# A decoder trunk on one core: the order of the small TensorE products in the RWKV tiles

## The chip, the core and the metric

The kernel runs on one core of a Trainium2 chip. The metric is device time in microseconds (us), the median of several executions. PE is TensorE, DVE is VectorE, ACT is ScalarE, POOL is GpSimd, and SP issues the DMAs.

## What is computed

Two layers on a residual stream of 256 tokens by 2048 channels: an RWKV-7 time mixing with a squared-ReLU MLP, then a latent attention with another MLP, each with norms and modulations made from a condition vector. The change lies in the time mixing. Cut to what matters, for each of 32 heads of 64 channels:

```python
def step(S, inp):
    r_t, w_t, k_t, v_t, kk_t, a_t = inp
    sa = jnp.einsum('bhvk,bhk->bhv', S, -kk_t)
    S = (S * w_t[:, :, None, :]
         + sa[..., None] * (kk_t * a_t)[:, :, None, :]
         + v_t[..., None] * k_t[:, :, None, :])
    y_t = jnp.einsum('bhvk,bhk->bhv', S, r_t)
    return S, y_t
```

The kernel does not walk the 256 tokens. It takes them in two chunks of 128, and within a chunk it solves for all the tokens at once: a triangular matrix of 128 by 128 per head and chunk is inverted, block by block.

## The kernel before

The program is one stream of Python calls; a planner in the framework orders each engine's instructions by their dependencies, its own estimate of times and the order of the calls, and puts the waits in. Each engine runs its list in that order.

**The RWKV stage** (here 230 to 754 us) runs 16 tiles, one for each pair of heads: `rwkv_tile(i)`, a generator whose yields are its steps. The loop at lines 905 to 928 keeps up to three tiles in flight, begins one every 9 steps, and between the steps draws the fill: the projections of the next tile (`project_rk`, lines 566 to 586: 48 products of 256 columns for each of two weight matrices go through `mm3w`, lines 213 to 215), and for the last tiles the first part of the output projection (`out_start`, lines 208 to 210). With every half of a weight tile that is loaded, ACT makes its high part (line 162), DVE its low part (line 163), and `pump` lets DVE do a share of the modulation sums of later layers (line 310). So PE's list in this stage mixes long projections with the many small products of the tiles.

A float32 product stands in the profile as two matrix instructions, called passes here. The steps of a tile that the change touches:

- `matrices` (lines 653 to 668), called twice for a tile, for `MB` and for `MK`: four products that contract over the 64 channels of one head. Head 0 lies on partitions 0 to 63, head 1 on 64 to 127; each head has a PSUM bank of its own (`pm[0]`, `pm[1]`, from the two banks of the pool `mm`). After them ACT copies head 0's bank, then head 1's (lines 663 and 666), with a mask by POOL between (line 667). Eight passes a group, 32 groups.
- the 32 by 32 blocks (lines 750 to 764): for each of four blocks of the diagonal four products, `A32` by `Tn` into `pW` (line 753), then `W` by `T16` into `pN` (line 762). The four blocks use four parts of the array (`tile_position=(32 * qi, 32 * qi)`) and four partition ranges of one bank; the block is the outer loop. 32 passes a group, 16 groups of each.
- the joins of two blocks (lines 773 to 788): for each half of the diagonal four products into `pW` (line 777) and a copy by ACT into `W32` (line 779), then four into `pN` (line 785) and a copy into `Tt` (line 787). The half is the outer loop, and the copy of the first half stands between the halves: both halves write one bank, and its next products come behind the copy. Eight passes a half.
- the state of the second chunk (lines 830 to 836): for each head two products into its 64 partitions of `psS` (lines 834 and 835), then a copy by ACT. Four passes a head.

Lines 793 to 806 (the 64 by 64 join), 825, 843 and 844 are not touched.

Of the kernel before, what the change touches and what calls it, by code (L numbers as in the profile page):

```python
# [20 lines left out]
P = 128  # L21
D = 2048
KT = D // P
T = 256
# [52 lines left out]
def trunk_kernel(ctx: ExitStack, tc: tile.TileContext, a, out, dbg=None):  # L77
    nc = tc.nc
    PE, DVE, ACT, POOL, SP = nc.tensor, nc.vector, nc.scalar, nc.gpsimd, nc.sync
# [52 lines left out]
    m16 = kc[:, o_ + 4 : o_ + 12]  # L132
    dlt = kc[:, o_ + 12 : o_ + 76].rearrange("p (m i) -> p m i", m=4)


    SEED, C0, C1 = 0x5F1FFFF9, 0.703952253, 2.38924456

# [216 lines left out]
    def big(name):  # L354
        return ap_.tile([P, 2, D], F32, tag="big", name=name)
# [22 lines left out]
    with ExitStack() as s0:  # L378
# [11 lines left out]
        with ExitStack() as s1:  # L390
# [5 lines left out]
            V = big("V")  # L396
# [28 lines left out]
            x = p2.tile([P, 2, D], F32, name="x")  # L425
# [36 lines left out]
            for cb in range(4):  # L462
# [13 lines left out]
                for kt in range(cb * 4, cb * 4 + 4):  # L476
# [8 lines left out]
                    h = p6.tile([P, T + 1], F32, tag="h", name="h")  # L485
# [4 lines left out]
                    for j in (3, 4, 5, 2, 0, 1):  # L490
# [10 lines left out]
                        if j == 3 or j == 4:  # L501
                            q = (kt % 4) * 2 * DL + (j - 3) * DL
                            wh, wl = lw_un["lwa"]
                            mm3w((pw if j == 3 else pa)[:DL], wh[:, q : q + DL], wl[:, q : q + DL], hi, lo, False, False)
                        elif j == 5:
                            q = (kt % 4) * 256
# [34 lines left out]
        with ExitStack() as s2:  # L541
# [9 lines left out]
            def tmp(tag, shape=(T,), bufs=1, dt=F32):  # L551
                return p5.tile([P, *shape], dt, tag=tag, name=tag, bufs=bufs)
# [8 lines left out]
            for j in range(LONG):  # L561
                Tt = p4.tile([P, 4, P], F32, name=f"Tt{j}")
# [25 lines left out]
            def rwkv_tile(i):  # L588
                K1 = DL + 1

                def tbank(name, k):
                    return banks[k].tile([P, 512], F32, tag=k, name=name)
# [7 lines left out]
                for z, (zh, zl) in enumerate(((zw_h, zw_l), (za_h, za_l))):  # L600
                    q = slice(z * P, (z + 1) * P)
# [34 lines left out]
                AR = tmp("AR", (2, 2, P), LONG)  # L636
# [14 lines left out]
                yield  # L651

                def matrices(lhs, M):
                    pm = [tbank("pm", "mm") for h in range(2)]
                    for c in range(2):
                        for h in range(2):
                            hp = slice(h * 64, h * 64 + 64)
                            PE.matmul(pm[h][:, c * T : (c + 1) * T], lhs[hp, c * P : (c + 1) * P],  # L658
                                      AR[hp, c, :, :].rearrange("p x t -> p (x t)"), start=True, stop=True)
                    for h in range(2):  # L660
                        if M is MB:
                            for c in range(2):
                                ACT.activation(M[:, h, c, :, :].rearrange("p x t -> p (x t)"), pm[h][:, c * T : (c + 1) * T],
                                               AF.Copy, scale=rinv[:, 2 * c + h : 2 * c + h + 1])
                        else:
                            ACT.copy(M[:, h].rearrange("p c x t -> p (c x t)"), pm[h])
                        POOL.affine_select(out=M[:, h], in_=M[:, h], pattern=[[0, 2], [1, 2], [1, P]], compare_op=ALU.is_ge,
                                           fill=0.0, base=-1, channel_multiplier=-1)

                MB = tmp("MB", (2, 2, 2, P), LONG)  # L670
                matrices(bt, MB)

                def At(m):
                    return MB[:, m // 2, m % 2, 0, :]
# [6 lines left out]
                bk = tmp("bk", bufs=2)  # L681
                for h in range(2):
                    q = slice(h * 64, h * 64 + 64)
# [4 lines left out]
                A32 = tmp("A32", (4, 32))  # L688
# [23 lines left out]

                MK = tmp("MK", (2, 2, 2, P), 2)
                matrices(kt_, MK)
                yield
                X = tmp("X", (4, 16), 2)
                ACT.copy(X, dlt)
                xt = tmp("xt", (4, 16))
                for j in range(15):
                    n = 15 - j  # L720
                    o = j * 16 + j + 1 if j < 8 else 128 + (j - 8) * 8 + j - 7
# [15 lines left out]
                for h in range(2):  # L737
                    vs = V[:, 0, i * P + h * 64 : i * P + h * 64 + 64]
# [3 lines left out]
                T16 = tmp("T16", (4, 32))  # L742
# [3 lines left out]
                quads = [slice(32 * q, 32 * q + 32) for q in range(4)]  # L746
                Tn = tmp("Tn", (4, 32))
                DVE.transpose(Tn.rearrange("p m t -> p (m t)"), T16.rearrange("p m t -> p (m t)"))
                yield
                pW = tbank("pW", "rt")  # L750
                for qi, q in enumerate(quads):
                    for m_ in range(4):
                        PE.matmul(pW[q, m_ * 16 : m_ * 16 + 16], A32[q, m_, :], Tn[q, m_, 0:16], start=True, stop=True,
                                  tile_position=(32 * qi, 32 * qi))
                W = tmp("W", (4, 32))
                POOL.memset(W[:, :, 16:32], 0.0)
                ACT.activation(W[:, :, 0:16], pW[:, 0:64].rearrange("p (m t) -> p m t", m=4), AF.Copy, scale=par[:, 1:2])
                yield
                pN = tbank("pN", "rt")
                for qi, q in enumerate(quads):  # L760
                    for m_ in range(4):
                        PE.matmul(pN[q, m_ * 32 : m_ * 32 + 32], W[q, m_, :], T16[q, m_, :], start=True, stop=True,
                                  tile_position=(32 * qi, 32 * qi))
                DVE.tensor_add(T16, pN[:, 0:P].rearrange("p (m t) -> p m t", m=4), T16)
                Tt = Tts[i % LONG]
                for q in quads:
# [2 lines left out]
                T32 = tmp("T32", (4, 32))  # L769
                W32 = T32  # L770
                DVE.transpose(T32.rearrange("p m t -> p (m t)"), T16.rearrange("p m t -> p (m t)"))
                yield
                pW = tbank("pW", "rt")
                for p_ in range(2):
                    e, o = slice(64 * p_, 64 * p_ + 32), slice(64 * p_ + 32, 64 * p_ + 64)
                    for m_ in range(4):
                        PE.matmul(pW[o, m_ * 32 : m_ * 32 + 32], At(m_)[e, o], T32[e, m_, :], start=True, stop=True,
                                  tile_position=(64 * p_, 64 * p_ + 32))
                    ACT.copy(W32[o], pW[o, 0:P].rearrange("p (m t) -> p m t", m=4))
                yield  # L780
                pN = tbank("pN", "rt")
                for p_ in range(2):
                    e, o = slice(64 * p_, 64 * p_ + 32), slice(64 * p_ + 32, 64 * p_ + 64)
                    for m_ in range(4):
                        PE.matmul(pN[e, m_ * 32 : m_ * 32 + 32], W32[o, m_, :], Tt[o, m_, o], start=True, stop=True,
                                  tile_position=(64 * p_ + 32, 64 * p_))
                    ACT.copy(Tt[e, :, o], pN[e, 0:P].rearrange("p (m t) -> p m t", m=4))
                yield

# [7 lines left out]
                pW = tbank("pW", "rt")  # L797
# [5 lines left out]
                pN = tbank("pN", "rt")  # L803
# [8 lines left out]
                for c in range(2):  # L812
                    if c:
                        pr = tbank("prhs", "rb")
                        PE.matmul(pr[:, :P], AR[:, c, 0, :], S, start=True, stop=False)
                        for h in range(2):
                            vs = V[:, c, i * P + h * 64 : i * P + h * 64 + 64]
                            PE.matmul(pr[:, h * 64 : h * 64 + 64], MK[:, h, c, 0, :], vs, start=False, stop=(h == 1))
                        rh = tmp("rh", (P,), 3)
                        ACT.copy(rh, pr[:, :P])  # L820
                        yield
                    pu = tbank("pu", "rb")
                    for h in range(2):
                        q = slice(h * 64, h * 64 + 64)
                        PE.matmul(pu[:, q], Tt[:, 2 * h + c, :], rh[:, q], start=True, stop=True)
                    U = tmp("U", (P,), 2)
                    ACT.copy(U, pu[:, :P])
                    yield
                    if c == 0:
                        psS = tbank("psS", "rb")  # L830
                        for h in range(2):
                            q = slice(h * 64, h * 64 + 64)
                            vs = V[:, 0, i * P + h * 64 : i * P + h * 64 + 64]
                            PE.matmul(psS[q, :64], bk[:, q], U[:, q], start=True, stop=False)
                            PE.matmul(psS[q, :64], bk[:, P + h * 64 : P + h * 64 + 64], vs, start=False, stop=True)
                            ACT.activation(S[q, q], psS[q, :64], AF.Copy, scale=sc[q, 1:2])
                    else:
                        PE.matmul(py[:, P:T], AR[:, c, 1, :], S, start=True, stop=False)
                    for h in range(2):
                        q = slice(h * 64, h * 64 + 64)  # L840
                        vs = V[:, c, i * P + h * 64 : i * P + h * 64 + 64]
                        o = py[:, c * P + h * 64 : c * P + h * 64 + 64]
                        PE.matmul(o, MB[:, h, c, 1, :], U[:, q], start=(c == 0), stop=False)
                        PE.matmul(o, MK[:, h, c, 1, :], vs, start=False, stop=(c == 0 or h == 1))
                    if c == 0:
                        yield
# [166 lines left out]
    x = xr  # L1013
# [550 lines left out]
```

## Time and profile before

| | |
|---|---|
| median of 3 runs | 2620.17 us (2618.22 to 2626.48) |
| profiled execution | 2610.6 us, span 2608.9 us |
| granted TensorE clock, mean | 0.989 |
| PE / PE weight load / DVE / ACT busy | 96% / 80% / 75% / 50% of the span |

The span is the time from the first to the last instruction of the profiled execution. A busy PE is a PE with at least one matrix instruction under way; the instructions are pipelined, so the durations of neighbours overlap, and how long a group holds the PE is read from its first start to the start of what follows it. The page names the chain of work that ended last and the groups of instructions by line; the views of the trace beside it are the busy time by stretch, the timeline of one engine (instructions of one line in a row are merged, xN), the groups of instructions and the waits.

### The profile page before, as it was taken

How to read it: one execution, taken by the hardware profiler on the slowest of the kernel's cores; microseconds unless marked ns; L12 is line 12 of the kernel's file. 1: busy time of each engine (PE TensorE's matmuls, PEld its weight loads, DVE VectorE, ACT ScalarE, POOL GpSimd, SP SyncE). 2: the span in 40 equal slices, each digit the busy share in tenths (PEclk: the TensorE clock that was granted, in tenths of full speed). 3: DMA queues.
4: the chain of work that ended last, by engine and by line, in shares of the span. 5: the costliest groups of instructions: out<-in, count | busy, mean ns of one | idle time of the engine just before them, and what ended most of it. 6: DMA issues, size and time to landing. Idle time of an engine off the chain costs nothing.

```text
span 2608.9 us, 39245 instructions
## 1 busy us (share of the span) xinstructions
PE 2510.7 (96%) x15048; PEld 2077.0 (80%) x15048; DVE 1950.6 (75%) x3823; ACT 1314.7 (50%) x2361; POOL 65.9 (3%) x150
## 2 busy tenths in 40 slices
PE   6998999999997999999999999999899999999998
PEld 3667888888776888888888878788788888888886
DVE  4797888888877788888888868777677655565555
ACT  4555666666745444444444446544544444444443
POOL 0000111011100000000000000000000000000000
PEclk9999999999999999999999999999999999999999
DMA  9755444444466588888888834657657555555553
GB/s 374 304 192 202 155 170 157 166 158 171 167 227 258 201 337 316 329 332 325 333 316 331 328 140 139 211 178 263 219 210 260 192 193 187 187 191 194 187 186 127
DMA packets 87885, 594.54 MB, mean 228 GB/s; under 512 B 10128, under 2 KB 14480, under 8 KB 16784
## 3 DMA queue, kind: packets, MB, share of 16 engines
q1 hardware_dynamic: 87696, 592.03, 62.9%
q8 instruction: 118, 1.93, 0.3%
q14 instruction: 71, 0.58, 0.1%
HBM read 589.89 MB, written 2.10 MB: 227 GB/s over the span
## 4 chain that ended last, share of the span: by engine, by line
PE 87%; DVE 7%; ACT 3%; DMA 2%; issue 1%; POOL 0%; SPq 0%; DVEq 0%; ACTq 0%
PE pup L223 17%; PE pd L208 9%; PE pd L210 9%; PE pd L209 9%; PE pup L224 9%; PE rk L213 2%; PE rk L215 2%; PE rk L214 2%; PE pm L658 2%; DVE wlo L163 2%; PE po L209 1%; PE po L210 1%; PE po L208 1%; PE pv L209 1%; PE pv L210 1%
## 5 line engine op out<-in xcount | busy, mean ns | idle before, releaser
L162 ACT CAST whi<-raw 128x1024 fp32r<-128x1024 f32 x729 | 743.7, 1023 | 882.7 <-PE pd L210 356.3
L163 DVE TENSOR_TENSOR wlo<-raw,whi 128x1024 fp32r<-128x1024 f32 x729 | 865.2, 1189 | 430.1 <-ACT whi L162 427.0
L223 PE MATMUL pup<-h,whi 128*128 128x512 f32 x1920 | 677.8, 398 | 0.0
L224 PE MATMUL pup<-h,wlo 128*128 128x256 f32 x1920 | 539.7, 281 | 0.0
L223 PEld LDWEIGHTS pup<-h,whi 128*128 128x128 f32 x1920 | 361.0, 188 | 88.2
L208 PE MATMUL pd<-whi,uh 128*128 128x512 f32 x1024 | 399.2, 390 | 0.0
L210 PE MATMUL pd<-whi,ul 128*128 128x512 f32 x1024 | 398.9, 390 | 0.0
L209 PE MATMUL pd<-wlo,uh 128*128 128x512 f32 x1024 | 398.8, 389 | 0.0
L310 DVE SCALAR_TENSOR_TENSOR raw<-raw,crow 128x1024 f32<-128x1024 f32 x320 | 388.5, 1221 | 10.5 <-DMA raw<-in_adat_dram 10.2
L224 PEld LDWEIGHTS pup<-h,wlo 128*128 128x128 f32 x1920 | 363.4, 189 | 0.5
L210 PEld LDWEIGHTS pd<-whi,ul 128*128 128x128 f32 x1024 | 192.3, 188 | 40.2
L208 PEld LDWEIGHTS pd<-whi,uh 128*128 128x128 f32 x1024 | 192.3, 188 | 39.9
L209 PEld LDWEIGHTS pd<-wlo,uh 128*128 128x128 f32 x1024 | 192.3, 188 | 39.5
L213 PE MATMUL rk<-xs,whi 128*128 128x256 f32 x512 | 155.2, 303 | 2.8 <-ACT rS L585 2.2
L215 PE MATMUL rk<-xs,wlo 128*128 128x256 f32 x512 | 149.6, 292 | 2.0 <-DVE wlo L163 2.0
L214 PE MATMUL rk<-xs,whi 128*128 128x256 f32 x512 | 147.1, 287 | 0.0
L213 PEld LDWEIGHTS rk<-xs,whi 128*128 128x128 f32 x512 | 98.5, 192 | 13.8 <-issue 8.9
L215 PEld LDWEIGHTS rk<-xs,wlo 128*128 128x128 f32 x512 | 98.4, 192 | 4.7 <-DVE wlo L163 2.8
L214 PEld LDWEIGHTS rk<-xs,whi 128*128 128x128 f32 x512 | 98.5, 192 | 0.9
L722 DVE TENSOR_TENSOR xt<-ar,X 128x60 f32<-128x60 f32 (+14 forms) x240 | 49.5, 206 | 17.5 <-ACT ar L711 14.8
L1180 DVE TENSOR_TENSOR ya<-pd,ya 128x512 f32<-128x512 f32 x96 | 61.5, 682 | 0.0
L209 PE MATMUL pv<-wlo,xsv 128*128 128x512 f32 x128 | 52.8, 413 | 5.5 <-DVE wlo L163 5.3
(431 smaller groups left out, 3671.3 us busy)
## 6 DMA issues: line engine op xcount, KB each, us to landing
raw<-in_adat_dram SPq DMA_DIRECT2D x160, 1024.0 KB, 6.9
raw<-in_up_dram SPq DMA_DIRECT2D x128, 1024.0 KB, 4.9
raw<-in_dn_dram SPq DMA_DIRECT2D x128, 1024.0 KB, 4.9
early<-in_ada_dram SPq DMA_DIRECT2D x17, 1024.0 KB, 11.6
raw<-in_wr_dram SPq DMA_DIRECT2D x16, 1024.0 KB, 4.9
raw<-in_wk_dram SPq DMA_DIRECT2D x16, 1024.0 KB, 5.0
raw<-in_wo_dram SPq DMA_DIRECT2D x16, 1024.0 KB, 5.8
raw<-in_mo_dram SPq DMA_DIRECT2D x16, 1024.0 KB, 4.9
```

The costliest lines, as they stand in the source:

```text
L162: ACT.copy(hi, x)
L163: return DVE.tensor_sub(lo, x, hi.bitcast(F32))
L208: PE.matmul(ps, lh, rh, start=start, stop=False)
L209: PE.matmul(ps, lh, rl, start=False, stop=False)
L210: PE.matmul(ps, ll, rh, start=False, stop=stop)
L213: PE.matmul(ps, wh, xh, start=start, stop=False)
L214: PE.matmul(ps, wh, xl, start=False, stop=False)
L215: PE.matmul(ps, wl, xh, start=False, stop=stop)
L223: PE.matmul(ps, hi[:, s], x2[:, kt].rearrange("p e t -> p (e t)"), start=(kt == 0), stop=False)
L224: PE.matmul(ps[:, T:], lo[:, s], x2[:, kt, 0, :], start=False, stop=(kt == KT - 1))
L310: DVE.scalar_tensor_tensor(raw[:, s], raw[:, s], 1.0, crow[:, s], ALU.mult, ALU.mult, accum_out=part[:, kt, half : half + 1])
L1180: DVE.tensor_add(y, pss[t], y)
```

## The change

A helper, `together`, is added. It issues the first of the products that it is given, and then the others in a block where each instruction on PE is ordered behind that first one and has high priority with the planner. All five places above go through it. In `matrices` head 1's product comes first in each pair, so the first product of a group waits for head 1's bank. In the 32 by 32 blocks the block becomes the inner loop. In the joins the half becomes the inner loop, and both copies come behind all the products of both halves. For `psS` the first products of both heads come first, then the second products of both, then both copies. The products, their sizes, and the number of instructions are the same.

```diff
--- before.py
+++ after.py
@@ -132,6 +132,16 @@
     m16 = kc[:, o_ + 4 : o_ + 12]
     dlt = kc[:, o_ + 12 : o_ + 76].rearrange("p (m i) -> p m i", m=4)
 
+
+    def together(*calls):
+
+        ins = calls[0]().ins
+        with tc.issue_after(ins), tc.high_priority():
+            for c_ in calls[1:]:
+                c_()
+
+    def product(*args, **kw):
+        return lambda: PE.matmul(*args, **kw)
 
     SEED, C0, C1 = 0x5F1FFFF9, 0.703952253, 2.38924456
 
@@ -651,12 +661,12 @@
                 yield
 
                 def matrices(lhs, M):
+
                     pm = [tbank("pm", "mm") for h in range(2)]
-                    for c in range(2):
-                        for h in range(2):
-                            hp = slice(h * 64, h * 64 + 64)
-                            PE.matmul(pm[h][:, c * T : (c + 1) * T], lhs[hp, c * P : (c + 1) * P],
-                                      AR[hp, c, :, :].rearrange("p x t -> p (x t)"), start=True, stop=True)
+                    hps = [slice(h * 64, h * 64 + 64) for h in range(2)]
+                    together(*(product(pm[h][:, c * T : (c + 1) * T], lhs[hps[h], c * P : (c + 1) * P],
+                                       AR[hps[h], c, :, :].rearrange("p x t -> p (x t)"), start=True, stop=True)
+                               for c in range(2) for h in (1, 0)))
                     for h in range(2):
                         if M is MB:
                             for c in range(2):
@@ -748,19 +758,17 @@
                 DVE.transpose(Tn.rearrange("p m t -> p (m t)"), T16.rearrange("p m t -> p (m t)"))
                 yield
                 pW = tbank("pW", "rt")
-                for qi, q in enumerate(quads):
-                    for m_ in range(4):
-                        PE.matmul(pW[q, m_ * 16 : m_ * 16 + 16], A32[q, m_, :], Tn[q, m_, 0:16], start=True, stop=True,
-                                  tile_position=(32 * qi, 32 * qi))
+                together(*(product(pW[q, m_ * 16 : m_ * 16 + 16], A32[q, m_, :], Tn[q, m_, 0:16], start=True, stop=True,
+                                   tile_position=(32 * qi, 32 * qi))
+                           for m_ in range(4) for qi, q in enumerate(quads)))
                 W = tmp("W", (4, 32))
                 POOL.memset(W[:, :, 16:32], 0.0)
                 ACT.activation(W[:, :, 0:16], pW[:, 0:64].rearrange("p (m t) -> p m t", m=4), AF.Copy, scale=par[:, 1:2])
                 yield
                 pN = tbank("pN", "rt")
-                for qi, q in enumerate(quads):
-                    for m_ in range(4):
-                        PE.matmul(pN[q, m_ * 32 : m_ * 32 + 32], W[q, m_, :], T16[q, m_, :], start=True, stop=True,
-                                  tile_position=(32 * qi, 32 * qi))
+                together(*(product(pN[q, m_ * 32 : m_ * 32 + 32], W[q, m_, :], T16[q, m_, :], start=True, stop=True,
+                                   tile_position=(32 * qi, 32 * qi))
+                           for m_ in range(4) for qi, q in enumerate(quads)))
                 DVE.tensor_add(T16, pN[:, 0:P].rearrange("p (m t) -> p m t", m=4), T16)
                 Tt = Tts[i % LONG]
                 for q in quads:
@@ -770,20 +778,19 @@
                 W32 = T32
                 DVE.transpose(T32.rearrange("p m t -> p (m t)"), T16.rearrange("p m t -> p (m t)"))
                 yield
+                halves = [(p_, slice(64 * p_, 64 * p_ + 32), slice(64 * p_ + 32, 64 * p_ + 64)) for p_ in range(2)]
                 pW = tbank("pW", "rt")
-                for p_ in range(2):
-                    e, o = slice(64 * p_, 64 * p_ + 32), slice(64 * p_ + 32, 64 * p_ + 64)
-                    for m_ in range(4):
-                        PE.matmul(pW[o, m_ * 32 : m_ * 32 + 32], At(m_)[e, o], T32[e, m_, :], start=True, stop=True,
-                                  tile_position=(64 * p_, 64 * p_ + 32))
+                together(*(product(pW[o, m_ * 32 : m_ * 32 + 32], At(m_)[e, o], T32[e, m_, :], start=True, stop=True,
+                                   tile_position=(64 * p_, 64 * p_ + 32))
+                           for m_ in range(4) for p_, e, o in halves))
+                for p_, e, o in halves:
                     ACT.copy(W32[o], pW[o, 0:P].rearrange("p (m t) -> p m t", m=4))
                 yield
                 pN = tbank("pN", "rt")
-                for p_ in range(2):
-                    e, o = slice(64 * p_, 64 * p_ + 32), slice(64 * p_ + 32, 64 * p_ + 64)
-                    for m_ in range(4):
-                        PE.matmul(pN[e, m_ * 32 : m_ * 32 + 32], W32[o, m_, :], Tt[o, m_, o], start=True, stop=True,
-                                  tile_position=(64 * p_ + 32, 64 * p_))
+                together(*(product(pN[e, m_ * 32 : m_ * 32 + 32], W32[o, m_, :], Tt[o, m_, o], start=True, stop=True,
+                                   tile_position=(64 * p_ + 32, 64 * p_))
+                           for m_ in range(4) for p_, e, o in halves))
+                for p_, e, o in halves:
                     ACT.copy(Tt[e, :, o], pN[e, 0:P].rearrange("p (m t) -> p m t", m=4))
                 yield
 
@@ -828,11 +835,12 @@
                     yield
                     if c == 0:
                         psS = tbank("psS", "rb")
-                        for h in range(2):
-                            q = slice(h * 64, h * 64 + 64)
-                            vs = V[:, 0, i * P + h * 64 : i * P + h * 64 + 64]
-                            PE.matmul(psS[q, :64], bk[:, q], U[:, q], start=True, stop=False)
-                            PE.matmul(psS[q, :64], bk[:, P + h * 64 : P + h * 64 + 64], vs, start=False, stop=True)
+                        heads = [slice(h * 64, h * 64 + 64) for h in range(2)]
+                        vs = [V[:, 0, i * P + h * 64 : i * P + h * 64 + 64] for h in range(2)]
+                        together(*(product(psS[q, :64], bk[:, q], U[:, q], start=True, stop=False) for q in heads),
+                                 *(product(psS[q, :64], bk[:, P + h * 64 : P + h * 64 + 64], vs[h], start=False, stop=True)
+                                   for h, q in enumerate(heads)))
+                        for q in heads:
                             ACT.activation(S[q, q], psS[q, :64], AF.Copy, scale=sc[q, 1:2])
                     else:
                         PE.matmul(py[:, P:T], AR[:, c, 1, :], S, start=True, stop=False)
```

## Rows read from the trace of the kernel before

**Rows 1.** The page: the chain that ended last, share of the span by engine.

```profile
PE 87%; DVE 7%; ACT 3%; DMA 2%; issue 1%; POOL 0%; SPq 0%; DVEq 0%; ACTq 0%
```

**Rows 2.** Stretches; columns: stretch, length, PE, PEld, DVE, ACT, POOL busy, clock, DMA.

```profile
230.00:754.00 524.00, 504.38 (x4804) 423.15 (x4803) 432.64 (x1412) 338.57 (x911) 60.12 (x108) 0.99 0.49 167
...
614.00:646.00 32.00, 31.09 (x307) 26.48 (x307) 27.73 (x92) 20.80 (x56) 3.52 (x7) 1.00 0.54 189
...
678.00:710.00 32.00, 29.78 (x252) 22.29 (x246) 28.33 (x100) 23.18 (x65) 7.09 (x8) 1.00 0.43 151
```

**Rows 3.** Groups of instructions of PE, 230 to 754 us; busy us, mean ns, idle before.

```profile
L658 PE MATMUL pm<-AR,kt 64*128 64x256 f32 x128 | 30.1, 418 | 0.0
L658 PE MATMUL pm<-AR,bt 64*128 64x256 f32 x128 | 25.4, 427 | 2.3 <-DVE AR L638 1.5 <-DVE bt L645 0.7
...
L762 PE MATMUL pN<-T,W 32*32 32x32 f32 x512 | 14.3, 194 | 0.0
```

**Rows 4.** Timeline of PE, 614 to 619 us; columns: start, us to the end.

```profile
614.84 1.13 PE L658 MATMUL pm<-AR,kt 64*128 64x256 f32 x6
615.89 0.43 PE L777 MATMUL pW<-T,MB 32*32 32x32 f32 x8
616.25 0.70 PE L658 MATMUL pm<-AR,kt 64*128 64x256 f32 x2
616.88 0.44 PE L872 MATMUL yt<-ident,tha 128*128 128x128 f32 x2
...
617.68 0.34 PE L777 MATMUL pW<-T,MB 32*32 32x32 f32 x5
617.84 0.21 PE L785 MATMUL pN<-Tt,T 32*32 32x32 f32 x1
617.86 0.19 PE L777 MATMUL pW<-T,MB 32*32 32x32 f32 x1
...
618.20 0.39 PE L213 MATMUL rk<-xs,whi 128*128 128x256 f32 x1
...
618.87 0.43 PE L785 MATMUL pN<-Tt,T 32*32 32x32 f32 x8
```

**Rows 5.** Timeline of PE: L658's first piece, a whole group, its last piece.

```profile
237.92 1.55 PE L658 MATMUL pm<-AR,bt 64*128 64x256 f32 x8 [1.55 <-DVE AR L638]
...
637.74 1.14 PE L658 MATMUL pm<-AR,bt 64*128 64x256 f32 x8
638.80 0.39 PE L213 MATMUL rk<-xs,whi 128*128 128x256 f32 x1
...
703.06 1.13 PE L658 MATMUL pm<-AR,kt 64*128 64x256 f32 x4
```

**Rows 6.** Timeline of PE around one group of line 762, 456 to 458 us.

```profile
456.66 0.28 PE L214 MATMUL rk<-xs,whi 128*128 128x256 f32 x1
456.87 0.90 PE L762 MATMUL pN<-T,W 32*32 32x32 f32 x32
457.70 0.39 PE L215 MATMUL rk<-xs,wlo 128*128 128x256 f32 x1
457.92 0.28 PE L213 MATMUL rk<-xs,whi 128*128 128x256 f32 x1
458.04 0.28 PE L214 MATMUL rk<-xs,whi 128*128 128x256 f32 x1
```

**Rows 7.** Groups of PE, 57.1 to 59.1 us: products in four column parts.

```profile
L287 PE MATMUL adap<-early,c 128*32 128x512 f32 x16 | 1.9, 598 | 0.0
```

**Rows 8.** Timeline of PE: the first head's products of psS, 280 us.

```profile
280.35 0.33 PE L834 MATMUL psS<-U,bk 128*64 128x64 f32 x2
...
280.72 0.43 PE L844 MATMUL py<-V,MK 128*128 128x64 f32 x2
```

**Rows 9.** Groups of ACT, 230 to 754 us: the copies that free the pm banks.

```profile
L663 ACT ACTIVATE MB<-pm,rinv 128x256 f32<-128x256 f32 x64 | 25.9, 473 | 27.5 <-PE pm L658 27.3
L666 ACT COPY MK<-pm 128x512 f32<-128x512 f32 x32 | 17.8, 587 | 6.0 <-PE pm L658 5.2
```

## Prediction

> **What bounds the kernel now.** First the page: the chain that ended last is 87% PE and 7% DVE [rows 1]. Then the stretches, since the change lies in one stage alone. [...] The reader should keep DVE in mind: in stretches of 32 us within the stage it reaches 27.73 and 28.33, a share of 0.87 to 0.885, and that is the most that any stretch I read shows [rows 2].
>
> Busy says little about how well PE is used, so the timeline comes third. A projection product is followed by the next after 0.12 us (457.92 to 458.04). The one ahead of a group of 32 by 32 blocks holds PE for 0.21 (456.66 to 456.87), and the first one behind it for 0.22 (457.70 to 457.92) [rows 6]. So each change of shape there and back costs 0.21 + 0.22 - 0.24 = 0.19 us, and a group that is cut in pieces pays it for each piece.
>
> Two more things are to be seen. Products in different parts of the array run side by side: a whole group of line 658 has eight passes of 0.42 us each on average [rows 3], and holds PE for 1.06 (637.74 to 638.80) [rows 5]. And products in one part do not: six passes and two passes of one group, in two pieces, hold it for 1.05 (614.84 to 615.89) and 0.63 (616.25 to 616.88) [rows 4], so the last two, with no partner, cost more than half of the whole group.
>
> **The change, part by part.** No instruction, transfer or wait of another engine is added; what changes is which passes stand next to each other on PE. Sixteen tiles run.
>
> *Line 658.* I counted 70 pieces in the timeline between the first and the last [rows 5] for 32 groups; 6 are whole. PE is busy in them for 30.1 + 25.4 = 55.5 us [rows 3]. A whole group is busy for 1.14 [rows 5], so 32 would take 36.5, 19.0 less. Of each of the 38 pieces too many, 0.08 us is tail that the next instruction overlaps (1.13 against 1.05 [rows 4]): 19.0 - 3.0 = 16.0. The 38 switches are worth up to 38 x 0.19 = 7.2; a third of the pieces stand beside other small products (as the two passes behind line 777 [rows 4]), so I take 5. Together 21. At least 10, if about half of the pieces stay apart; at most 23.
>
> *Lines 753 and 762.* A group of 32 passes now holds PE for 0.83 (456.87 to 457.70) [rows 6]; I take the same for line 753. Eight passes in one part, line 777, hold it for 0.36 (615.89 to 616.25) [rows 4]. With four parts side by side a group needs those 0.36 and 0.03 for the later starts, an estimate from the 0.02 us between two rows of different parts (617.84 and 617.86). Four parts do go on together, for column parts: sixteen passes of 0.60 take 1.9 us [rows 7]. Gain (0.83 - 0.39) x 32 = 14.1. If only two parts go together, 2 x 0.36 = 0.72 and the gain is 3.5.
>
> *Lines 777 and 785.* Three pieces for each tile now: half of line 777 at 0.36, its other half mixed with the first half of line 785 at 0.52 (617.68 to 618.20), and the rest, eight passes again, at 0.36 [rows 4]: 1.24. Afterwards line 777 in one piece with two parts side by side, 0.37. Line 785 reads what two copies by ACT make one after the other, so the planner may issue one half's products and then the other's; I take 0.52 for it, and 0.37 as its best. Gain 0.35 x 16 = 5.6, and one piece fewer, 0.19 x 16 = 3.0. The range is 3 to 11. That both copies come after all the products costs nothing, as the second half no longer waits for the first copy.
>
> *Lines 834 and 835.* Each head's four passes hold PE for 0.37 (280.35 to 280.72) [rows 8], twice for a tile, in two pieces. Side by side in two column parts about 0.38 in all: 0.36 x 16 = 5.8, and 3.0 for the switch. The range is 3 to 9.
>
> *Head 1's bank first.* The first product of a group now waits for the bank that ACT copies last. Head 0's products could have begun one copy sooner; the wait hides behind the projections, which are on hand in most of the stage. Without that cover it costs at most half of the copies' time, (25.9 + 17.8) / 2 = 21.9 us [rows 9]. I take nothing, because the planner has projection products to put in front.
>
> The sum is 21 + 14 + 8.6 + 8.8 = 52 us of PE, 57 at best; at worst 10 + 3.5 + 3 + 3 = 19.5, less 21.9 for the banks, about nothing.
>
> **What becomes of it.** The stage of 524 us would fall to 472 if PE alone counted. Then DVE, whose work stays, would be busy for 432.6 of 472, a share of 0.92. The most that a row shows is 0.885, which gives 432.6 / 0.885 = 489, a gain of 35. I stand nearest to that row and take 36: the DVE's waits for PE get a little shorter too, since a join has one round trip between PE and ACT less. Against the profiled execution's own 2610.6 us this is 2575. That execution lay 9.6 below the median of the runs, so for the median 2620.2 - 36 = 2584.
>
> **The rivals.** All times are medians. About 0.3%, 8 us, is what a measurement of this kernel can tell from no change.
>
> 1. *The forecast:* most of the gain on PE arrives and DVE takes the rest: 25 to 48 us, 2572 to 2595. Chance 0.55.
> 2. *PE's gain arrives whole.* DVE has no trouble at 0.92, as much of its idle time is waiting for these very groups. 2620 - 52 = 2568, down to 2563 with the best sum. Against it: no row of the stage has such a share. Chance 0.18.
> 3. *DVE, or the chain of a tile through PE, ACT and DVE, keeps the pace.* A third to a half of the PE time comes back as waits: 10 to 24 us, 2596 to 2610. For it: DVE's share. Against it: PE's idle time in the stage is small now, 524 - 504. Chance 0.16.
> 4. *The change does not do what it says.* High priority is a matter of the planner's own estimates: if it still finds other work ready first, the pieces stay, and only a few us are left, 2612 to 2620. Chance 0.06.
> 5. *Blocks that share a bank collide; slower.* Four row parts write one bank, pW or pN, in turns. If a pass had to wait for the end of one in another row part, 0.19 us (line 762's mean [rows 3]), each of the 16 products of a 32-pass group would cost 0.19 + 0.03 instead of sharing: 16 x 0.22 = 3.5 against 0.83, +2.7 x 32 = +86. The eight products each of lines 777 and 785 would cost 3.5 for a tile against 1.24, +36. Less the 30 of the two other places: about +92, 2712. It decides from the point where such a wait eats the sum, 52 us over 768 products, about 0.07 us each. Against it: line 785 starts at 617.84 in one half of the array while line 777 has five passes under way in the other from 617.68, and the next pass of line 777 follows 0.02 later [rows 4]; and a group of 32 passes in 0.83 us leaves 0.026 for each [rows 6], less than the 0.36 / 8 = 0.045 of a single part, so blocks already overlap in one bank. Chance 0.05.
>
> [...]
>
> **How the numbers follow.** Likeliest: 2584. The range of 8 in 10 takes the first case, the second down to 2560, and the third up to 2608; it leaves out the last two and the edges. Faster by over 0.3%: 0.55 + 0.18 + 0.16 = 0.89. Within 0.3%: 0.06. Slower: 0.05.
>
> **What would show it.** In the changed profile line 658 should have about 32 pieces of eight passes at 1.06; lines 753 and 762 32 passes in about 0.4; line 777 sixteen in one piece at 0.37; lines 834 and 835 one piece a tile. The stage should take about 488 us, with DVE's share near 0.885 and more idle time on PE than the present 20 us. I am wrong if the groups are whole and the stage is as long as before (then PE was not the bound), or if the groups of 32 passes do not get shorter (then four row parts do not go together).

## The result, and the profile after

The changed kernel takes 2594.31 us (2586.83 to 2599.04, four runs), the kernel before 2623.10 in four runs beside it: a ratio of 0.9889 [0.9859, 0.9919], 28.8 us less where 36 were forecast. The profiled execution took 2599.04 us, its span 2597.3. All products of the five places now stand on line 144 (`product`); other lines of the tiles have moved down by seven to ten.

The page: the busy time of each engine, and the chain that ended last, by engine:

```profile
PE 2487.8 (96%) x15048; PEld 2060.5 (79%) x15048; DVE 1945.7 (75%) x3823; ACT 1312.5 (51%) x2361; POOL 70.9 (3%) x150
...
PE 77%; DVE 8%; ACT 4%; issue 1%; DMA 1%; POOL 0%; DVEq 0%; ACTq 0%
```

Stretches of the changed kernel, columns as in [rows 2]: the same 524 us as there, the whole stage (first product of line 223 to the last of the output projection's first part), one stretch to come back to, and two ordinary ones:

```profile
230.00:754.00 524.00, 491.30 (x4923) 417.21 (x4922) 443.81 (x1445) 347.19 (x927) 65.08 (x108) 0.98 0.51 179
218.00:780.00 562.00, 527.14 (x5113) 447.68 (x5112) 468.91 (x1478) 361.23 (x946) 65.08 (x108) 0.98 0.53 187
395.00:417.00 22.00, 19.76 (x119) 16.32 (x120) 12.92 (x43) 11.19 (x31) 0.10 (x1) 0.53 0.41 146
...
518.00:550.00 32.00, 29.98 (x357) 25.69 (x345) 28.80 (x101) 22.74 (x66) 4.49 (x8) 1.00 0.56 200
...
678.00:710.00 32.00, 30.10 (x255) 21.54 (x254) 28.82 (x91) 19.75 (x55) 3.87 (x6) 1.00 0.50 169
```

The whole stage of the kernel before:

```profile
212.00:796.00 584.00, 561.02 (x5121) 471.11 (x5119) 472.84 (x1478) 364.12 (x947) 60.12 (x108) 0.99 0.52 180
```

The stage fell from 584 to 562 us, with 6.8 us of it at a granted clock of 0.5 before and 23.9 after; less half of that time (an estimate, explained below) the fall is about 31 us. PE's busy time fell by 33.9 us, DVE's by 3.9; PE stands still for 34.9 us of the stage now (562.00 - 527.14) and stood still for 23.0 before. The timeline of PE in the changed kernel shows what became of the pieces (columns as in [rows 4]):

```profile
302.04 0.44 PE L144 MATMUL pW<-Tn,A 32*32 32x16 f32 x32
302.41 0.38 PE L223 MATMUL rk<-xs,whi 128*128 128x256 f32 x1
...
303.36 0.45 PE L144 MATMUL pN<-T,W 32*32 32x32 f32 x32
303.75 0.38 PE L225 MATMUL rk<-xs,wlo 128*128 128x256 f32 x1
...
305.04 0.44 PE L144 MATMUL pW<-T,MB 32*32 32x32 f32 x16
305.41 0.39 PE L224 MATMUL rk<-xs,whi 128*128 128x256 f32 x1
...
306.08 0.24 PE L144 MATMUL pN<-Tt,T 32*32 32x32 f32 x2
306.25 0.38 PE L225 MATMUL rk<-xs,wlo 128*128 128x256 f32 x1
306.56 0.43 PE L144 MATMUL pN<-Tt,T 32*32 32x32 f32 x14
306.93 1.13 PE L144 MATMUL pm<-AR,kt 64*128 64x256 f32 x8
307.90 0.38 PE L800 MATMUL pT<-ident,Tt 64*64 64x64 f32 x4
```

A group of 32 passes holds PE for 0.37 (302.04 to 302.41) and 0.39, where it was 0.83 [rows 6]; a group of 16 for 0.37; line 658's eight passes for 0.97. Old line 658 is still cut in two of its 32 groups, and old line 785 in 7 of 16 tiles: two passes, projections, then the other 14. Counted over the stage, in pieces and in time held (first start of a piece to the first start of what follows, with any idle time between):

| old line | pieces | PE held, us |
|---|---|---|
| 658 | 70 to 34 | 51.0 to 36.4 |
| 753 | 16, 16 | 13.0 to 5.9 |
| 762 | 16, 16 | 13.2 to 7.3 |
| 777 | 80 to 16 | 9.7 to 7.2 |
| 785 | 80 to 23 | 10.3 to 8.8 |
| 834, 835 | 32 to 16 | 13.7 to 6.4 |

That is 38.9 us less. (Before, one half's products of line 777 alternate with the other half's of line 785, which makes the 80 short pieces of each.) The chain inside the stage, by line, says who took over; first the kernel before (212 to 796), then the changed one (218 to 780):

```profile
by line: PE rk L213 10.1%; PE rk L215 9.1%; PE rk L214 8.8%; PE pm L658 7.2%; PE ar L710 3.9%; DMA raw<-in_adat_dram 3.6%; DVE wlo L163 3.0%; PE py L843 2.5%; PE pu L825 2.5%; PE pos L210 2.4%; PE py L844 2.3%; PE pos L209 2.3%; PE pos L208
```

```profile
by line: DVE wlo L173 6.0%; DVE raw L320 5.4%; PE rk L223 5.0%; PE rk L224 4.9%; PE rk L225 4.8%; PE ar L720 4.2%; issue 3.5%; PE pos L220 3.0%; PE pos L219 2.8%; PE pos L218 2.7%; ACT whi L172 2.6%; DVE X L733 2.3%; DMA raw<-in_adat_dram 2
```

The two longest single lines are now DVE's: the low parts of the weights (line 173) and the modulation sums (line 320). PE still has most of the chain. Added up from the trace over all lines of the stage, its share fell from 78% to 53%, DVE's rose from 9% to 26% and ACT's from 7% to 12%.

**A second scale.** The stretch from 395 to 417 us has a granted clock of 0.53. The traces of the two kernels show a granted clock of 1.00 or 0.50 and nothing between; here it is 0.50 for 20.5 of the 22 us, and a group of 16 passes is busy for 0.91 us there, where another took 0.44 (last section). Time at 0.50 is called time at half clock below. Such time varies from run to run and from kernel to kernel, so each kernel is given twice: the median as measured, and the mean of its runs less half of their time at half clock, which is 2 x (1 - mean clock) x span, also as a mean. The second number, which the expectations call the time at full clock, is an estimate. A straight line through the runs of one kernel gives 0.2 to 0.5 us of time for a microsecond at half clock, so half is the highest price that the runs show, and small differences on this scale hang on it.

| kernel | median, us | ratio to before | at half clock, us | less half of it |
|---|---|---|---|---|
| before, four series | 2620.9 to 2624.8 | | 88 to 96 | 2576 to 2578 |
| the change | 2594.3 | 0.9889 [0.9859, 0.9919] | 91 | 2548 |
| mat_only | 2634.8 | 1.0039 [1.0025, 1.0054] | 124 | 2571 |
| blk_only | 2614.3 | 0.9968 [0.9958, 0.9979] | 96 | 2566 |
| join_only | 2623.0 | 0.9994 [0.9977, 1.0011] | 101 | 2571 |
| st_only | 2642.0 | 1.0070 [1.0046, 1.0094] | 141 | 2570 |
| short_sums_before | 2627.0 | 1.0031 [1.0012, 1.0049] | 107 | 2576 |
| short_sums_after | 2567.8 | 0.9789 [0.9770, 0.9808] | 78 | 2529 |
| order_only | 2591.6 | 0.9879 [0.9860, 0.9899] | 70 | 2557 |
| head0_first | 2592.9 | 0.9877 [0.9858, 0.9897] | 85 | 2549 |
| late_half_first | 2596.4 | 0.9884 [0.9865, 0.9904] | 92 | 2549 |
| pool_lo_after | 2620.1 | 0.9981 [0.9966, 0.9995] | 117 | 2561 |
| pool_lo_before | 2667.2 | 1.0142 [1.0111, 1.0172] | 151 | 2588 |
| st_filled | 2658.5 | 1.0131 [1.0105, 1.0156] | 102 | 2606 |

### The profile page after: what moved, and what is told of

The parts are those of the page before. It is cut to its first block, busy times and chain, and to the rows that moved or that the text cites. A ratio compares the mean times of both kernels' runs of the same rounds, so it can differ in the third digit from the quotient of the medians.

```text
span 2597.3 us, 39264 instructions
## 1 busy us (share of the span) xinstructions
PE 2487.8 (96%) x15048; PEld 2060.5 (79%) x15048; DVE 1945.7 (75%) x3823; ACT 1312.5 (51%) x2361; POOL 70.9 (3%) x150
## 4 chain that ended last, share of the span: by engine, by line
PE 77%; DVE 8%; ACT 4%; issue 1%; DMA 1%; POOL 0%; DVEq 0%; ACTq 0%
PE pup L233 17%; PE pd L218 9%; PE pd L220 9%; PE pd L219 9%; PE pup L234 9%; DVE wlo L173 2%; DVE raw L320 1%; PE po L219 1%; PE po L220 1%; PE po L218 1%; PE rk L223 1%; PE rk L224 1%; PE rk L225 1%; PE pl L218 1%; PE ar L720 1%
```

## The experiments

The theory: the packed groups free PE as the sum says, and DVE, next in line, gives a third of it back as waits. Its rivals: the gain is the sum of what the parts bring alone, with no engine in the way; it comes from the togetherness or from the leading bank, not from the order; DVE's load is not what matters, but the length of a tile's chain; and, once the first runs were there, that the clock decides what is left of each part.

**Each part alone.** Each kernel is the one before with `together`, `product` and one part of the change (the edits are cut to their first lines):

```diff
--- mat_only: in matrices
-                    for c in range(2):
-                        for h in range(2):
+                    together(*(product(pm[h][:, c * T : (c + 1) * T], lhs[hps[h], c * P : (c + 1) * P],
--- blk_only: the 32 by 32 blocks
-                for qi, q in enumerate(quads):
-                    for m_ in range(4):
+                           for m_ in range(4) for qi, q in enumerate(quads)))
--- join_only: the joins
-                for p_ in range(2):
-                    e, o = slice(64 * p_, 64 * p_ + 32), slice(64 * p_ + 32, 64 * p_ + 64)
+                           for m_ in range(4) for p_, e, o in halves))
--- st_only: psS
-                        for h in range(2):
+                        together(*(product(psS[q, :64], bk[:, q], U[:, q], start=True, stop=False) for q in heads),
...
```

> The kernel before with the new order of line 658 alone. Theory A (PE is the bound as long as DVE is at 0.83 of the stage, so a part alone brings all that it saves on PE; the whole change brought less because DVE comes next): 21 us less than before, a ratio of 0.992. Rival B (a group put together waits at the head of PE's list for its latest input, so each part gives back a share of its own): 11 to 12 us less, 0.9955. Rival C (the tiles' chain of products and copies sets the pace; line 658 lies little on it): 0 to 5 us less, 0.998 or above. All: nearly every group in one piece of eight passes at 1.06 us.

> The kernel before with the new order of the 32 by 32 blocks (lines 753 and 762) alone. Theory A: 14 us less, 0.9945. Rival B: 7 to 8 us less, 0.997. Rival C: these groups are links of the tiles' chain, 0.44 us shorter each, so about 14 us here too. All: 32 passes in 0.37 to 0.39 us.

> The kernel before with the new order of the joins (lines 777 and 785) alone. Theory A: 8 to 9 us less, 0.9965. Rival B: 4 to 5 less, 0.998. Rival C: the chain of a tile loses one round trip between PE and ACT, about 1 us for each of 16 tiles, so 10 to 16 us less, 0.995.

> The kernel before with the new order of lines 834 and 835 alone. Theory A: 9 us less, 0.9965. Rival B: 4 to 5 less, 0.998. Rival C: a round trip less between the heads, about 1 us for each of 16 tiles, 10 to 16 us less, 0.995. The sum of the four ratios' gains is 52 us by theory A, about 29, as the whole change brought, by rival B.

As measured, the four together lose: +12.1, -8.5, +0.3 and +19.3 against the 2622.7 of the kernel before beside them, +23 in sum, where the whole change gains 29. Only `blk_only` came out near a theory, rival B; that a part would be slower was in none of them. In the traces each part holds PE as in the whole change (36.3 us for line 658, 12.1 for the blocks, 15.4 for the joins, 6.3 for psS), so each does give PE time. On the second scale they gain 7, 12, 7 and 8 against 2578.3, in sum 35, the whole 30; the stages of the profiled executions, reckoned in the same way, give 10, 14, 12 and 12, in sum 48, the whole 32. Three of the parts come with 101 to 141 us at half clock instead of 90. That this time eats their gain fits, but is not shown: it rests on the price of half. At 0.3 instead, `mat_only` and `st_only` would still be 2 and 4 us slower than before. Line 658 alone has its 34 pieces, yet gains no more than 7 to 10: PE's idle time in its stage is 35.0 us against 23.0.

**DVE made lighter, before and after.** Line 310 (320 in the changed kernel) takes a quarter of its columns; three quarters of the modulation sums are left out, in the whole kernel.

```diff
-                        DVE.scalar_tensor_tensor(raw[:, s], raw[:, s], 1.0, crow[:, s], ALU.mult, ALU.mult,
+                        DVE.scalar_tensor_tensor(raw[:, half * 1024 : half * 1024 + 256], raw[:, half * 1024 : half * 1024 + 256], 1.0, crow[:, half * 1024 : half * 1024 + 256], ALU.mult, ALU.mult,
```

> The kernel before with line 310 on a quarter of its columns (256 of 1024): it leaves out three quarters of the modulation sums, and so some 75 to 80 us of DVE's 473 in the RWKV stage. [...] Theory D (PE bounds the stage before the change, DVE after it): little change, 0 to 10 us less at full clock. Rival W (DVE already sets the pace in places, by what it makes late for PE): 15 us or more less.

> The changed kernel with the same quarter of line 310, the rest of the modulation sums left out. Theory D (DVE took the missing 22 of 52 us): the distance to the run before it, both at full clock, grows from the 30 us of the two whole kernels to 42 to 52. Rival W (the rest is lost to the order of PE's list and the chain of a tile through PE and ACT, not to DVE's load): the distance stays at 25 to 35.

Before the change a lighter DVE brings nothing (ratio 1.0031; 0.7 us on the second scale). After it, it brings 26 us (19). So the change is worth 59 us between these two (47 on the second scale) and 29 (30) with the full sums. The stage of each, columns as in [rows 2], without and with the change:

```profile
213.00:809.00 596.00, 576.84 (x5105) 483.36 (x5104) 416.46 (x1478) 360.35 (x945) 47.27 (x108) 0.97 0.49 175
```

```profile
222.00:758.00 536.00, 515.41 (x5098) 441.04 (x5097) 410.11 (x1477) 357.32 (x944) 49.95 (x108) 0.99 0.54 194
```

In the second the stage is 26 us shorter than with the full sums (536 against 562), and PE's idle time is 20.6 us where the change with full sums has 34.9. That DVE takes the rest is shown. Whether it is DVE's load in sum, or the long sums that stand in its list ahead of a tile's short steps, is not: the edit shortens both.

**The order without the togetherness; the other head's bank first.** `order_only` keeps the new order of calls and drops the ordering behind the first product and the high priority; `head0_first` lets head 0 lead.

```diff
-        ins = calls[0]().ins
-        with tc.issue_after(ins), tc.high_priority():
-            for c_ in calls[1:]:
-                c_()
+        for c_ in calls:
+            c_()
--- head0_first
-                               for c in range(2) for h in (1, 0)))
+                               for c in range(2) for h in (0, 1)))
```

> The changed kernel with its order of products, but without the issue-after edge and the high priority: the planner may cut groups again. If the order alone is what packs the blocks and halves (theory O), lines 753 and 762 stay near 0.39 us and the loss is confined to line 658, whose groups fall in pieces again: 2551 to 2558 at full clock, a ratio to before of 0.990 to 0.994. If the togetherness is needed everywhere (theory T), all groups are cut and 5 to 10 us of the gain are left, 0.997.

> The changed kernel with head 0 leading in line 658, as before the change; all else as changed. Theory H (the first product must wait for the bank that comes free last, or the group is cut): line 658 is in 55 to 65 pieces instead of about 34, and 7 to 15 us of the gain go: 2555 to 2563 at full clock, ratio to before 0.992 to 0.995. Rival: the high priority keeps the group whole whichever head leads: 2548 at full clock, 0.989.

Without togetherness line 658 stays in 71 pieces and holds PE for 51.1 us. Two pieces of one group, from the timeline of `order_only`:

```profile
306.49 0.70 PE L145 MATMUL pm<-AR,kt 64*128 64x256 f32 x4
307.15 0.44 PE L881 MATMUL yt<-ident,tha 128*128 128x128 f32 x2
...
309.24 0.49 PE L145 MATMUL pm<-AR,kt 64*128 64x256 f32 x2
```

The other places hold it for 5.9, 6.2, 5.9, 8.2 and 6.1 us, as in the changed kernel or less. The time is the same, 0.9879 against 0.9889; theory O had the groups and the time on the second scale right, but not the measured ratio (0.990 to 0.994). On the second scale togetherness is worth 9 us, which would mean that it loses them to time at half clock, 91 against 70 us; that too rests on the price of half. With head 0 in the lead the pieces stay 34 and the time is the same: which bank leads does not matter.

**Line 785 whole.**

```diff
-                           for m_ in range(4) for p_, e, o in halves))
+                           for m_ in range(4) for p_, e, o in halves[::-1]))
```

> The changed kernel with the second half leading in line 785, so that the first product waits for the copy by ACT that is made last. Theory: the 7 groups of line 785 that were cut behind their first product, and the 5 whole ones that stood for the second copy, become whole at 0.37 us: about 4 us of PE, 2 to 4 less at full clock (2548 for the changed kernel), ratio to before 0.987 to 0.989. Rival (DVE paces the stage, so PE time saved comes back as waits): no difference, 0.989.

All 16 groups are whole, as here (timeline of this kernel), and the time is the same, as the rival had it. The gain expected, 2 to 4 us, is about as small as the noise.

```profile
303.86 0.44 PE L144 MATMUL pN<-Tt,T 32*32 32x32 f32 x16
304.23 1.13 PE L144 MATMUL pm<-AR,kt 64*128 64x256 f32 x8
```

**DVE relieved by POOL.** The subtractions of 256 columns (32 of `wlo`, 16 of `ol`) go to POOL, in both kernels.

```diff
-    def hilo(hi, lo, x):
+    def hilo(hi, lo, x, by=DVE):
...
-        return DVE.tensor_sub(lo, x, hi.bitcast(F32))
+        return by.tensor_sub(lo, x, hi.bitcast(F32))
...
-            hilo(hi[:, :m], lo[:, :m], raw[:, c0 : c0 + m])
+            hilo(hi[:, :m], lo[:, :m], raw[:, c0 : c0 + m], POOL if n == T else DVE)
...
```

> The changed kernel with 48 subtractions of 256 columns in the RWKV stage (the low parts of the small weights, line 173 called for 256 columns, and of the tiles' outputs) moved from DVE to POOL, which is busy for only 65 of 524 us: about 20 us less for DVE. Theory D (DVE bounds the stage after the change): 8 to 16 us less at full clock, 2532 to 2540, ratio to before 0.982 to 0.986. Rival S (POOL is slow on them, or what waits for them becomes late): nothing gained, 0.989 or above.

> The kernel before with the same 48 subtractions on POOL. Theory D: DVE is not the bound there, so within 4 us of before at full clock (2578), ratio 0.998 to 1.002. Rival W (DVE is in the way there too): 8 us less or more, 0.997 or below.

Beside the kernels that they came from, these lost 0.9% and 1.4%. The first is rival S; so great a loss in the kernel before was in neither theory. Groups by line, first of the changed kernel by shape, then of `pool_lo_after`:

```profile
L173 DVE TENSOR_TENSOR wlo<-raw,whi 128x256 fp32r<-128x256 f32 x32 | 13.4, 420 | 5.1 <-ACT whi L172 5.1
```

```profile
L173 POOL TENSOR_TENSOR wlo<-raw,whi 128x256 fp32r<-128x256 f32 x32 | 27.4, 856 | 108.4 <-ACT whi L172 89.8 <-PE pT L800 4.8 <-DVE rsy L168 3.5
...
L733 DVE TENSOR_TENSOR X<-X,xt 128x60 f32<-128x60 f32 (+14 forms) x240 | 55.0, 229 | 3.3
```

POOL takes 856 ns for what DVE does in 420, and the small DVE steps of the triangle solve take 229 ns instead of 205. The stage of `pool_lo_after`, columns as in [rows 2]:

```profile
215.00:808.00 593.00, 549.61 (x5108) 465.23 (x5107) 473.70 (x1430) 362.15 (x946) 105.19 (x156) 0.95 0.50 177
```

DVE has 48 instructions fewer, but its busy time did not fall (473.70 us against 468.91), as the others took longer; PE's idle time rose to 43.4 us. So DVE did not become lighter, and this pair does not test the theory; that a lighter DVE pays rests on the short sums alone.

**More projections among the small products.** `st_only`, of the four parts the one with most time at half clock, with unused products added ahead of each of the seven steps (the first is shown):

```diff
                 pW = tbank("pW", "rt")
+                for _ in range(3): PE.matmul(pW[:, T:], sg_h[:, 0, :P], sg_h[:, 1, :], start=True, stop=True)
```

> [...]

The theory is that the clock falls where few projections stand among the small products. Time at half clock fell from 141 to 102 us, inside the 105 that it wanted; the time was 16.5 us longer than `st_only`, where it allowed 10, and on the second scale 36 longer. Stages of `st_only`, then of `st_filled`, where the clock rises from 0.92 to 0.96:

```profile
217.00:831.00 614.00, 586.31 (x5102) 487.56 (x5101) 469.07 (x1478) 362.22 (x944) 59.45 (x108) 0.92 0.48 170
```

```profile
216.00:842.00 626.00, 611.83 (x5453) 522.80 (x5452) 485.36 (x1478) 366.10 (x946) 55.33 (x108) 0.96 0.47 168
```

The rival, that the fall has nothing to do with what stands there, wanted 130 us at half clock, which did not come, and a price of 20 to 40 us, which nearly did. The added products are no remedy, and they support the theory only in part: time at half clock is left in 4 of the 16 solves (6 in `st_only`), and these four hold 37 to 48 projection passes besides the added products.

## Why the prediction was right

- **What bounds the kernel, and what comes next.** Right. PE was busy for 0.96 of the 524 us and DVE for 0.83 [rows 2]; PE's share of the chain shrank from 87% [rows 1] to 77%, DVE's in the stage rose from 9% to 26%, and the short sums show the rest: with DVE light the change is worth 47 to 59 us, about the 52 of the sum; with DVE's full load 17 of the 47 are lost, where the prediction gave up 16 of 52.
- **The share of 0.885.** Right as a size, wrong as a ceiling. In 13 stretches of 32 us from 262 to 710, without the one at half clock, DVE is busy for 28.2 us on average, 0.88 (26.85 and 0.84 in the 14 from 276 to 724 before), and the fullest reach 0.90. Over the whole stage it is 468.91 of 562, 0.83 (472.84 of 584 before, 0.81), as its ends and the stretch at half clock are in it.
- **Line 658, 21 us.** The pieces and the time held came as priced (34 pieces, 14.6 us less against 16.0). That this part alone gains 7 on the second scale, and loses 12 as measured, is the missed size. PE's idle time in that stage is 12 us longer than before, which fits that much of the 14.6 went into waits; which waits these are is not shown. The 5 us for its switches don't show: PE's busy time in the stage fell by 33.9 us, or by about 42 once half of the 17 us that the changed stage has more at half clock (23.9 against 6.8) is taken off, and 39 of these are time held, which leaves about 3 for the 11 us of switches priced over all places.
- **Lines 753 and 762, 14 us.** Held 13.0 us less; 12 alone on the second scale. Four row parts go together: 0.37 and 0.39 where 0.39 was taken.
- **Lines 777 and 785, 8.6 us.** Held 4.0 less against 5.6; 7 alone on the second scale. Line 785 at 0.52 lay between its two cases, 0.37 whole and 0.17 + 0.37 in two pieces; it did not matter.
- **psS, 8.8 us.** Held 7.3 less (5.8 priced), 0.40 a tile where 0.38 was taken; 8 alone on the second scale.
- **Head 1's bank, nothing.** Right: `head0_first`. Nor was the togetherness needed for the measured time: the new order alone gives it, with line 658 in 71 pieces. So the largest term of the sum, 21 us, adds nothing to the measured gain (9 us on the second scale); that a sum with it in came so near is partly luck.
- **The rival of the collision** fell. Here 32 passes in four row parts of one bank took 0.37 us, 0.012 each, so for blocks in different partitions of a bank the measurement decides against it.
- **The time.** 2594 against 2584: 3 us because before's median is 2623.1 in these runs, 7 because the gain is 28.8, not 36. The time lies just inside the forecast's own case (2572 to 2595). What the prediction left out altogether is the clock. It cancelled in the whole (91 us at half clock, as before), but not in the parts; that it cancelled is luck.

## What to carry to other kernels

Order products so that neighbours lie in different parts of the array: where four 32 by 32 parts took turns in the inner loop, a group took less than half its time (0.37 to 0.39 us against 0.83), and for these groups the order of the calls alone was enough (5.9 and 6.2 us for the 16 groups of each in `order_only`). Ask which engine is next, and how far it is from full: here DVE, busy for 0.83 of the stage, took a third of PE's gain. Judge parts of such a change together, and read the granted clock beside each time: two of these parts were slower alone and the whole is faster.

## What was not expected of the hardware

The clock fell in the middle of a stage in which PE was busy for over 90% (527.14 of 562 us). The timeline of PE in the changed kernel ahead of the stretch at 0.53 (in brackets the idle time just before, and what ended it):

```profile
392.93 0.44 PE L144 MATMUL pW<-Tn,A 32*32 32x16 f32 x32 [0.93 <-DVE rst L159]
...
394.09 0.45 PE L144 MATMUL pN<-T,W 32*32 32x32 f32 x32
395.63 0.66 PE L880 MATMUL yt<-ident,tha 128*128 128x128 f32 x2 [1.09 <-DVE tha L876]
...
397.29 0.64 PE L144 MATMUL pW<-T,MB 32*32 32x32 f32 x16
398.29 0.91 PE L144 MATMUL pN<-Tt,T 32*32 32x32 f32 x16 [0.36 <-ACT T L787]
```

PE stood still for 0.93 and 1.09 us with small products around, and from then to about 416 us ran at a granted clock of 0.50: the group of 16 passes is busy for 0.91 where another took 0.44. The number of projection passes that stand inside a tile's triangle solve (old line 753 to the last product of old line 805) does not settle it. In `order_only` the solves with 6 to 15 of them have no such time; in `short_sums_before`, `pool_lo_after`, `pool_lo_before` and `st_filled` sixteen solves with 33 to 51 of them have it. What tips it stays open.
